# A hybrid mLSTM and chunk-MLP layer on one core: when weight blocks are cut in two parts and when their loads begin

## The chip, the core and the metric

The kernel runs on one core of a Trainium2 chip. The metric is device time in microseconds of one execution, the median over several runs. TensorE (PE in the rows) does the matrix products, with the loading of its stationary operand counted apart (PEld); VectorE (DVE) and ScalarE (ACT) do elementwise work and empty PSUM, GpSimd (POOL) does some elementwise work in SBUF, and SyncE's queue (SP) issues all the DMAs. Each engine takes its own instructions in order; an instruction that has to wait holds back everything behind it on that engine.

## What is computed

One inference step of one layer, on a prompt of 2048 rows of 1024 features and on eight single sample rows. Cut to what matters here:

```
h      = rmsnorm(x)
proj   = h @ w_in                      # 1024 -> 10248 columns: q, k, v, o, z_a, gates, u, vb, z_b, gate_a, gate_b
q, k   = silu(causal_conv(q, k))
hm     = mlstm(q, k, v, ...)           # 4 heads x 256, chunks of 128 rows
y_a    = sigmoid(o) * rmsnorm(hm) * silu(z_a)
y_b    = u * (tril(w_s) @ layernorm(vb) + b_s) * silu(z_b)
merged = sigmoid(gate_a) * (y_a @ w_pa) + sigmoid(gate_b) * (y_b @ w_pb)
x      = x + rmsnorm(merged @ w_out)
x      = x + sigmoid(x @ w_ple_gate) * rmsnorm(p @ w_ple)
```

All of it is in float32, and the matmuls must keep about that precision.

## The kernel before

**Passes, units, products.** The prompt is taken in NP = 4 passes of 512 rows (the sample rows ride along in pass 1). In each pass the big products with weights are 28 units in the order of `PASS`: four times v, qk, og, gg (one head each), four times ub, and two each of pa, pb, wo and wg. Each unit is a product of a 1024 by 512 weight with the pass's 512 rows, done in Strassen's way: 2 by 2 blocks, seven block products in place of eight. A block is 512 by 256 (one SBUF tile of 128 partitions by 1024 floats, 512 KB). The seven products of a unit take the weight blocks in the order A11, A12, S2, S3, S1, A22, S4 (`ORDER`; S1 to S4 are sums of raw blocks). So there are 28 x 7 = 196 products in a pass and 784 in all.

**Cutting.** To keep precision, each operand is cut into a high part (`whi`, a copy by ACT into the type fp32r, line 124) and a low part (`wlo`, block minus high part, by DVE, line 129). A product is 24 matmuls: for each of 4 slices of 128 and each of 2 halves, high x high, high x low, low x high. They stand in `run_unit` at lines 490 (results with rows of x on the partitions) and 493 (the other way round, printed as rhi/whi and so on).

**Where blocks come from.** In pass 0 the raw blocks are loaded, the sums are made by DVE, and all are kept in DRAM. In passes 1 to 3, S2, S1 and S4 (`CUT_KEPT`) are loaded ready cut, as a pair of tiles, high and low. The other four of each unit (A11, A12, S3, A22; "raw blocks" below) are loaded as one raw tile (`wraw`) and cut anew. All these tiles come from one pool of 13 buffers (`w`). A tile is handed the buffer of a tile that was used up; its first write waits until the last reader of that one is done. Buffers are handed out in the order in which tiles are asked for.

**The schedule.** `Stream` holds the list of all products. Just ahead of the matmuls of product t, `run_unit` calls `reach_high(t + 1)`, where `n` is `t + 1`: first the high copies up to product `n + CUT - 1` = t + 2, then the loads up to product `n + LOAD - 1` = t + 7 (in pass 0 up to `n + 4`). In the middle of the product's matmuls it calls `reach_low`, which asks for the low tiles of the high copies just made and has DVE make them. After the product come the copies out of PSUM (`snap` and `consumer`: tiles `s`, `u`, and the names of the results), and then a step of whatever runs beside it (attention, convolution, the cutting of the other operand in `build`, the fetching of it back from DRAM in `from_dram`: tiles `blk`, `rhi`, `rlo`). The tool that builds the program keeps roughly this order on each engine, but may move instructions.

Of the kernel before, what the change touches and what calls it, by code (L numbers as in the profile page):

```python
# [74 lines left out]
def tile_layer(ctx: ExitStack, tc: tile.TileContext, I, O):  # L75
# [46 lines left out]
    def copy(out, in_, scale=None):  # L122
        if scale is None:
            S.activation(out, in_, AF.Copy)  # L124
        else:
            S.activation(out, in_, AF.Copy, scale=scale)
# [129 lines left out]
    class Stream:  # L256


        CUT, SUM, LOAD = 2, 3, 7

        def __init__(self):
            self.items = [(p, u, n) for p in range(NP) for u in PASS for n, *_ in order(u)]
# [58 lines left out]

        def reach_high(self, n):
            end = len(self.items)
            while self.split < min(end, n + self.CUT):
                key = self.items[self.split]
                self.split += 1
                if key in self.ready:
                    continue
                hi = self.tile(key[1], "whi", F32R)
                copy(hi, self.raw[key])  # L330
                self.high[key] = hi
            n = min(n, end - 1)
            while self.loaded < min(end, n + (self.LOAD if self.items[n][0] else 5)):
                self.load(*self.items[self.loaded])
                self.loaded += 1
# [1424 lines left out]
```

## Time and profile before

| what | value |
|---|---|
| median of 3 runs | 2886.32 us (2886.23 to 2891.51) |
| the profiled execution | 2878.66 us, of which the span from first to last instruction 2877.0 us |
| TensorE busy (matmul) | 2703.2 us, 94% of the span |
| VectorE, ScalarE, GpSimd busy | 2143.5, 1540.1, 512.8 us |
| mean DMA rate | 268 GB/s |
| pass 0, passes 1 to 3 in the trace | 0 to 798, 798 to 1553, 1553 to 2213, 2213 to 2877 us |

The pass borders are the starts of the first weight product of each pass, read from the trace. Idle time that a wait shows is that of the engine named first. A row of the waits gives who waited, for whom, the total, how often, and the longest. A row of the timeline gives start, duration, engine, line, operation, tiles, and in brackets the idle time ahead of it with what ended it.

### The profile page before, as it was taken

What the parts mean: (1) busy time and instruction counts of PE and PEld (TensorE: products, weight loads), DVE (VectorE), ACT (ScalarE), POOL (GpSimd) and SP (SyncE); (2) the same over time, 40 slices, a digit from 0 to 9 for tenths busy, and PEclk for the clock granted to TensorE, in tenths of its full rate; (3) what the DMA queues carried; (4) which work ended last, traced back from release to release, by engine and by line L of the source; (5) the groups of instructions that cost most, each with busy time, mean ns of one, the idle gap of its engine ahead of it and who ended that gap; (6) DMA issues with size and microseconds to landing.
All of it is one profiled execution on the core that took longest, in us unless ns stands there. A gap on an engine that the chain in (4) does not pass through costs nothing. (4 is left out here: it accounts for less than half of the span.)

```text
span 2877.0 us, 56022 instructions
## 1 busy us (share of the span) xinstructions
PE 2703.2 (94%) x21835; PEld 2639.0 (92%) x21835; DVE 2143.5 (75%) x3513; ACT 1540.1 (54%) x2668; POOL 512.8 (18%) x557
## 2 busy tenths in 40 slices
PE   6999999888899999999999999999999999999998
PEld 6899989888789899989889999999998999999898
DVE  8888888888977667766868766567678766665767
ACT  5555646445645555544456655564356545554445
POOL 3333332334310000101020100101111010101110
PEclk9999999899999999999999999999999999999999
DMA  6567667867777888889878777779878787788886
GB/s 223 220 249 273 242 235 267 295 253 255 262 257 249 287 267 273 276 272 328 285 250 294 254 260 257 253 258 322 311 277 298 241 268 262 252 272 279 317 283 231
DMA packets 268628, 770.37 MB, mean 268 GB/s; under 512 B 30066, under 2 KB 89338, under 8 KB 268355
## 3 DMA queue, kind: packets, MB, share of 16 engines
q1 hardware_dynamic: 268362, 766.79, 77.0%
q8 instruction: 172, 2.82, 0.4%
q14 instruction: 94, 0.76, 0.1%
HBM read 595.29 MB, written 171.53 MB: 267 GB/s over the span
## 5 line engine op out<-in xcount | busy, mean ns | idle before, releaser
L493 PE MATMUL acc<-rhi,whi 128*128 128x256 f32 (+1 forms) x4480 | 1289.6, 288 | 30.9 <-ACT s L124 8.9
L493 PE MATMUL acc<-rhi,wlo 128*128 128x256 f32 (+1 forms) x4480 | 1276.5, 286 | 43.1 <-DVE wlo L129 34.1
L493 PE MATMUL acc<-rlo,whi 128*128 128x256 f32 (+1 forms) x4480 | 1275.2, 285 | 0.0
L493 PEld LDWEIGHTS acc<-rhi,wlo 128*128 128x128 f32 x4480 | 859.3, 192 | 50.3 <-DVE wlo L129 39.6
L493 PEld LDWEIGHTS acc<-rhi,whi 128*128 128x128 f32 x4480 | 860.2, 192 | 41.6 <-ACT s L124 10.3
L493 PEld LDWEIGHTS acc<-rlo,whi 128*128 128x128 f32 x4480 | 859.4, 192 | 0.0
L129 DVE TENSOR_TENSOR wlo<-wraw,whi 128x1024 fp32r<-128x1024 f32 (+1 forms) x462 | 597.7, 1297 | 179.2 <-PE acc L493 77.2
L124 ACT ACTIVATE whi<-wraw 128x1024 fp32r<-128x1024 f32 (+1 forms) x504 | 530.1, 1055 | 349.6 <-PE acc L493 209.4
L490 PE MATMUL acc<-whi,rhi 128*128 128x256 f32 (+1 forms) x1792 | 517.7, 290 | 20.7 <-ACT rhi L124 6.7
L490 PE MATMUL acc<-wlo,rhi 128*128 128x256 f32 (+1 forms) x1792 | 512.0, 287 | 16.2 <-DVE wlo L129 14.1
L490 PE MATMUL acc<-whi,rlo 128*128 128x256 f32 (+1 forms) x1792 | 511.8, 286 | 6.3 <-DVE rlo L129 6.2
L490 PEld LDWEIGHTS acc<-whi,rhi 128*128 128x128 f32 x1792 | 346.1, 193 | 28.0 <-ACT rhi L124 9.6
L490 PEld LDWEIGHTS acc<-wlo,rhi 128*128 128x128 f32 x1792 | 345.1, 193 | 19.8 <-DVE wlo L129 16.9
L490 PEld LDWEIGHTS acc<-whi,rlo 128*128 128x128 f32 x1792 | 346.3, 193 | 8.2 <-DVE rlo L129 8.2
L124 ACT ACTIVATE u<-acc 128x512 f32<-128x512 f32 (+1 forms) x272 | 138.9, 517 | 209.8 <-PE acc L493 156.8
L129 POOL TENSOR_TENSOR wlo<-wraw,whi 128x512 fp32r<-128x512 f32 (+1 forms) x84 | 149.0, 1794 | 291.6 <-ACT whi L124 209.5
L124 ACT ACTIVATE s<-acc 128x512 f32<-128x512 f32 (+1 forms) x136 | 69.4, 513 | 79.3 <-PE acc L493 47.2
L790 POOL TENSOR_TENSOR so<-so,sz 128x512 f32<-128x512 f32 (+1 forms) x32 | 60.2, 1880 | 289.7 <-ACT so L774 171.9
L1293 POOL TENSOR_TENSOR yb<-yb,ub 128x512 f32<-128x512 f32 (+1 forms) x32 | 57.1, 1799 | 293.8 <-DVE ub L1291 127.0
L241 POOL TENSOR_SCALAR aab<-au 128x2 f32<-128x2 f32 x32 | 8.5, 266 | 481.6 <-DVE au L883 481.6
L869 DVE SCALAR_TENSOR_TENSOR cext<-cext,fst,smp 128x258 f32<-128x258 f32 x128 | 60.5, 479 | 36.1 <-PE smp L806 36.0
L720 POOL COPY halo<-raw 128x3 f32<-128x3 f32 x64 | 27.5, 454 | 284.8 <-DVE raw L139 154.7
(365 smaller groups left out, 3899.0 us busy)
## 6 DMA issues: line engine op xcount, KB each, us to landing
wraw<-in_w_main SPq DMA_DIRECT2D x351, 512.0 KB
xh<-xh SPq DMA_DIRECT2D x32, 512.0 KB
sg<-sgm SPq DMA_DIRECT2D x24, 512.0 KB
gsig<-sg SPq DMA_DIRECT2D x24, 512.0 KB
x<-in_x_prompt SPq DMA_DIRECT2D x16, 512.0 KB
ya<-ya SPq DMA_DIRECT2D x32, 256.0 KB
xr<-in_x_prompt SPq DMA_DIRECT2D x32, 256.0 KB
pg<-pg SPq DMA_DIRECT2D x32, 256.0 KB
```

The lines of the kernel that those rows point to most:

```text
L124: S.activation(out, in_, AF.Copy)
L129: eng.tensor_tensor(lo, full, hi.bitcast(F32), op=ALU.subtract)
L241: G.tensor_scalar(out, ms, EPS, None, op0=ALU.add)
L490: T.matmul(outs[s], x[:, kt, s * P:(s + 1) * P], wt[:, kt, :], start=first, stop=last, skip_group_check=not opens)
L493: T.matmul(outs[s], wt[:, kt, s * P:(s + 1) * P], x[:, kt, :], start=first, stop=last, skip_group_check=not opens)
L720: G.tensor_copy(halo[:, ct, :], x[:, TP:TP + 3])
L790: G.tensor_tensor(so[:, s], so[:, s], sz[:, s], op=ALU.mult)
L869: V.scalar_tensor_tensor(cext[:, h, kt, :], cext[:, h, kt, :], gt.fst[:, h, self.c:self.c + 1], p3, op0=ALU.mult, op1=ALU.add)
L1293: G.tensor_tensor(y[:, :, l, :], y[:, :, l, :], ub[:, :, l, :], op=ALU.mult)
```

## The change

Two numbers of `Stream`'s schedule. In products of passes 1 to 3 the high copies (and with them the low parts) are asked for one product further ahead: up to t + 3 in place of t + 2. And the loads in these passes begin one product less far ahead: up to t + 6 in place of t + 7. Pass 0 keeps its two and its five.

```diff
-        CUT, SUM, LOAD = 2, 3, 7
+        CUT, SUM, LOAD = 2, 3, 6
...
         def reach_high(self, n):
             end = len(self.items)
-            while self.split < min(end, n + self.CUT):
+            while self.split < min(end, n + self.CUT + (self.items[min(n, end - 1)][0] > 0)):
                 key = self.items[self.split]
                 self.split += 1
                 if key in self.ready:
```

No instruction is added or taken away, and the pool keeps its 13 buffers.

## Rows read from the trace of the kernel before

**Rows 1.** The page: span, busy time of the engines, granted clock.

```profile
span 2877.0 us, 56022 instructions
...
PE 2703.2 (94%) x21835; PEld 2639.0 (92%) x21835; DVE 2143.5 (75%) x3513; ACT 1540.1 (54%) x2668; POOL 512.8 (18%) x557
...
PEclk9999999899999999999999999999999999999999
```

**Rows 2.** Busy time by pass: stretch, length, engines (instructions), clock, DMA share, GB/s.

```profile
0.00:798.00 798.00, 696.92 (x5399) 676.73 (x5400) 690.12 (x912) 444.24 (x712) 286.76 (x234) 0.94 0.70 252
798.00:1553.00 755.00, 726.35 (x5819) 694.28 (x5818) 543.30 (x1136) 402.48 (x779) 80.94 (x132) 0.98 0.81 275
1553.00:2213.00 660.00, 642.49 (x5327) 636.96 (x5326) 462.94 (x744) 356.94 (x606) 73.26 (x103) 0.98 0.81 277
2213.00:2877.00 664.00, 637.41 (x5296) 630.98 (x5295) 447.18 (x724) 336.39 (x573) 71.81 (x88) 0.99 0.79 269
```

**Rows 3.** Waits of PE in passes 1 to 3 (798 to 2877).

```profile
PE acc L493 <- DVE wlo L129: 18.2, 14, 3.3
PE smp L1599 <- DVE xq L1591: 6.9, 4, 1.8
PE acc L490 <- DVE wlo L129: 6.2, 5, 3.1
...
PE acc L493 <- ACT u L124: 3.9, 7, 0.7
...
PE acc L493 <- ACT whi L124: 2.1, 2, 1.0
...
PE acc L490 <- DVE rlo L129: 1.5, 2, 1.2
```

**Rows 4.** Waits of DVE, ACT and the SP queue in passes 1 to 3.

```profile
DVE wlo L129 <- PE acc L493: 77.2, 56, 3.9
...
ACT whi L124 <- PE acc L493: 192.0, 109, 5.2
...
SPq L117 <- DVE wlo L129: 515.9, 255, 6.7
SPq L117 <- PE acc L493: 453.7, 276, 5.0
```

**Rows 5.** Instructions on tile wraw: duration min/median/max in ns, first and last start.

```profile
L124 ACT ACTIVATE whi<-wraw x504: 1039/1057/1087, 10.4 to 2853.7; 128x1024 fp32r<-128x1024 f32 x162, 128x1040 fp32r<-128x1040 f32 x6
L129 DVE TENSOR_TENSOR wlo<-wraw,whi x462: 1149/1222/2348, 16.0 to 2855.7; 128x1024 fp32r<-128x1024 f32 x148, 128x1040 fp32r<-128x1040 f32 x6
```

**Rows 6.** DVE and ACT timeline in a regular stretch of pass 1.

```profile
1175.07 1.22 DVE L129 TENSOR_TENSOR wlo<-wraw,whi 128x1024 fp32r<-128x1024 f32 x1 [0.16 <-issue]
...
1178.09 1.23 DVE L129 TENSOR_TENSOR wlo<-wraw,whi 128x1024 fp32r<-128x1024 f32 x1 [0.96 <-PE acc L493]
...
1175.18 1.06 ACT L124 ACTIVATE whi<-wraw 128x1024 fp32r<-128x1024 f32 x1 [2.40 <-PE acc L493]
```

**Rows 7.** Line 493 alone in a dense stretch: length, PE and PEld busy (x), clock, DMA.

```profile
1177.80:1195.30 17.50, 17.50 (x148) 17.50 (x147) 1.00 0.82 276
```

**Rows 8.** PE timeline: waits at the pass border and in three merge stretches.

```profile
812.51 0.58 PE L490 MATMUL acc<-wlo,rhi 128*128 128x260 f32 x1 [3.13 <-DVE wlo L129]
...
1371.14 0.49 PE L493 MATMUL acc<-rhi,wlo 128*128 128x260 f32 x1 [3.31 <-DVE wlo L129]
...
2044.44 0.58 PE L493 MATMUL acc<-rhi,wlo 128*128 128x256 f32 x1 [3.21 <-DVE wlo L129]
...
2712.56 0.48 PE L493 MATMUL acc<-rhi,wlo 128*128 128x256 f32 x1 [1.77 <-DVE wlo L129]
```

**Rows 9.** SP queue, ACT and DVE in the merge stretch of pass 2.

```profile
2030.69 3.75 SPq L117 DMA_DIRECT2D blk<-yb  x4
2034.54 0.40 SPq L117 DMA_DIRECT2D wraw<-in_w_main  x1
...
2039.68 1.06 ACT L124 ACTIVATE rhi<-blk 128x1024 fp32r<-128x1024 f32 x1 [1.59 <-DMA blk<-yb]
...
2040.77 1.22 DVE L129 TENSOR_TENSOR rlo<-blk,rhi 128x1024 fp32r<-128x1024 f32 x1 [4.09 <-ACT rhi L124]
2042.03 1.22 DVE L136 TENSOR_TENSOR blk<-blk 128x1024 f32<-128x1024 f32 x1
2043.17 1.22 DVE L129 TENSOR_TENSOR wlo<-wraw,whi 128x1024 fp32r<-128x1024 f32 x1
```

**Rows 10.** All engines in the merge stretches of passes 2 and 3, columns as in the second group.

```profile
2034.00:2046.00 12.00, 8.34 (x63) 7.93 (x62) 6.58 (x7) 3.66 (x4) 0.00 (x0) 0.90 1.02 414
2701.00:2713.00 12.00, 9.77 (x79) 9.37 (x78) 5.47 (x6) 5.21 (x6) 0.00 (x0) 0.99 1.02 403
```

**Rows 11.** A landing in an ordinary stretch: issue on the SP queue, first use by PE.

```profile
2743.40 0.43 SPq L117 DMA_DIRECT2D prow<-in_p_prompt  x1
...
2748.44 0.41 PE L1454 MATMUL smp<-ident,prow 128*128 128x128 f32 x2 [1.58 <-DMA prow<-in_p_prompt]
```

## The prediction

> **What bounds the kernel now.** I read the page first: PE is busy for 94% of the span, at nine tenths of its clock or more in every slice [rows 1]. So the time is PE's own work plus what PE stands still, and only the second can move here, as no matmul is added or taken away. Next the busy time by pass [rows 2]: in pass 0 PE stands 798.0 - 696.9 = 101 us, in passes 1 to 3 it stands 28.7 + 17.5 + 26.6 = 73 us. The change acts in passes 1 to 3 alone, so 73 us, 2.5% of the time, is all that it could ever win.
>
> Then what PE waits for in those passes [rows 3]. The largest entry is the low part of a weight block: 18.2 us in 14 waits at line 493 and 6.2 us in 5 at line 490, together 24.4 us in 19 waits, none over 3.3 us. The high part costs 2.1 us at line 493. The rest is the chain of the output stage (6.9 us), copies out of PSUM (u, 3.9 us) and the like, which do not hang on the cut.
>
> Why is a low part late? The waits of the other engines [rows 4] show that DVE, ahead of a low part, stood 77.2 us in 56 waits for PE, and ACT, ahead of a high part, 192.0 us in 109. Nothing that these read comes from PE; what they wait for is the buffer to write in, which a product must set free first. A regular stretch shows the rhythm [rows 6]: low parts start 3.02 us apart (1175.07, 1178.09), the second after 0.96 us of standing for PE, and each takes 1.2 us [rows 5]. A product is 24 matmuls; 148 of them took 17.5 us [rows 7], so one product takes 24 x 0.118 = 2.8 us, or 2.9 with the gaps. So a low part starts as a product ends, and the product after the next one needs it one product later: the cushion is 2.9 - 1.2 - 0.2 = 1.5 us (0.2 for handing on). Any delay of DVE beyond 1.5 us stops PE.
>
> **The change, part by part.** *Cutting one product further ahead.* The number of cuts is the same, some 336 in passes 1 to 3 (3 passes, 28 units, 4 raw blocks), with the same 1.06 us on ACT and 1.22 us on DVE [rows 5], so no engine gets more work. Each low part gets one product more before it is needed: the cushion grows from 1.5 to about 4.4 us. A wait of x us today was a low part late by x beyond its cushion, so every wait up to 2.9 us should go and the two of 3.3 and 3.2 us [rows 8] should leave 0.4 and 0.3.
>
> That holds only if the buffers allow it, so I counted the tiles held once a product's requests are made: two for each product that is cut, three for the raw block being cut, and one (raw) or two (pair) for each block loaded ahead. Before: 4 for products t and t + 1, then block t + 2, then five loads. For t = A11, A12, ..., S4 that is 13, 14, 13, 14, 13, 14, 15, on average 13.7, against 13 buffers. That fits the rows: with the pool always full the low parts wait for the end of a product. After: 6 for three cut products, block t + 3, then three loads: 14, 12, 13, 12, 13, 14, 12, on average 12.9. So one load less pays for one cut more. High parts should find a buffer free without waiting for PE, and only two low parts of four (those of S3 and A12) still wait for a product's end, which now leaves them 4.4 us.
>
> So of the 24.4 us, what goes? The wait of 3.13 us at 812.51 [rows 8] stays: it belongs to the second product of pass 1, and the deeper cut begins with requests made at the pass border, too late for it. 24.4 - 3.1 = 21.3. Of these, 3.31 + 3.21 + 1.77 = 8.3 us lie in the three merge stretches [rows 8]. There the low part stood behind a cut of the other operand (`rlo<-blk`), which DVE could not start for 4.09 us because `blk` came late [rows 9]. The low part now goes ahead of that, but the next one ahead may be held by its own load (below), so I take half, 4.1. Of the other 13.0 us I take four fifths, 10.4: where DVE is behind by its own work, what PE meets next is a copy out of PSUM, such as u with waits of up to 0.7 us [rows 3]. Of the 2.1 us for high parts I take half, 1.0. Sum: 4.1 + 10.4 + 1.0 = 15.5 us.
>
> *Loads one product later.* The number of DMAs is the same. On the SP queue each weight load moves one product back, past whatever is asked for in between (attention's rows, gates, `blk`, stores); these gain, for the queue stood 515.9 us for low parts and 453.7 us for PE [rows 4], mostly for buffers of loads asked for too early. A raw block was loaded seven products ahead and copied by ACT two ahead: five products, 14.5 us, for the transfer. Now it is six and three: three products, 8.7 us. The nearest rows for a landing: a small one in an ordinary stretch took 2743.40 to 2748.44, 5.0 us [rows 11]; the first of four 512 KB transfers in a merge stretch, where the DMA share is 1.02, took 2030.69 to 2039.68, 9.0 us [rows 9, 10]. So ordinarily 3.7 us are left and the cost is nothing; in the merge stretches a landing can be 0.3 us late or more. Below: nothing. Above: the third rival. I take nothing beyond the half already given away, as a late copy has the new cushion before PE stops. Pairs loaded ready cut lose a product too, and keep six, 17.4 us, which is far above 9.0.
>
> *Order on the engines.* The builder may move instructions, and a new schedule may be laid out otherwise in places. No row prices that; I put nothing, and it is one reason for the width.
>
> The sum against the profiled execution: 2878.66 - 15.5 = 2863.2 us (its span of 2877.0 would be 2861.5). The median of the runs shown lies 7.7 us above that execution, so for the median 2886.3 - 15.5 = 2870.8, say **2871 us**.
>
> **The rivals.** *The wait comes back as a wait for buffers (nothing gained, 2886 us).* If low parts still get their buffer only as the product before their use ends, the 24.4 us stay. For it: 77.2 us in 56 waits on PE show that buffers, not raw data, held DVE [rows 4]. Against it: the count, 12.9 tiles in place of 13.7. The Trainium skill, Perfetto Trace Analysis, section Optimization Strategy, says that a gap which repeats on the engine that should be full can mean that there isn't enough SBUF for the next tile. By that rule a longer lead in the same 13 buffers would win nothing; the trace agrees that the pool was the brake, but in the count the load depth pays for the lead.
>
> *The time is given back at the next late thing (2881 us).* DVE is busy 543.3 of 755 us in pass 1 and near 70% in passes 2 and 3 [rows 2]. Where it is simply behind, an earlier low part means a later copy out of PSUM, behind it in DVE's queue. If two thirds of the 15.5 us come back so, 5 us are left: 2886.3 - 5 = 2881. For it: DVE worked without a gap from 2040.77 until the low part was done, just ahead of the wait of 3.21 us [rows 8, 9]. Against: it idles for some 30% of these passes.
>
> *Raw blocks land too late (slower, 2896 us).* The point that decides is a landing longer than 8.7 us. Place: the two fetches of an operand in each pass, whose four `blk` transfers of 512 KB now go ahead of a weight load that used to precede them. At 403 GB/s [rows 10] those four take 4 x 0.524 / 403 = 5.2 us, on top of 5.0 [rows 11]: 10.2 us, 1.5 too late. ACT stands in its copy, DVE in the low part behind it, and with them the copies out of PSUM that PE needs for its next bank. On four blocks of each of six fetches that is 24 x 1.5 = 36 us, and the 4.1 us counted as won there are lost as well: 2886.3 - 11.4 + 36 = 2911 if PE pays all, 2893 if it pays half; I put the case at 2896. For it: DMA shares of 1.02 and the 9.0 us [rows 9, 10]. Against: there are only a few such stretches, and PE has the new cushion and other PSUM banks before it has to stop.
>
> **How the numbers follow.** The spread of the runs shown, 2886.23 to 2891.51, is 0.2%, or 5.8 us: less than that cannot be told from no change. Chances: the forecast 0.65, the buffer rival 0.08, given back 0.14, late landings 0.13. The first lies under 2880.5, that is faster: 0.65; the next two are within 0.2%: 0.22; the last is slower: 0.13. The forecast's own range: at best all of 21.3 + 2.1 us goes, and the 3.9 and 1.5 us of u and rlo [rows 3] with it, 28.8 us, 2857; at worst half of the 15.5 comes, 2879. To hold 8 in 10 the range takes in the two cases of no difference and stops short of the slower one: 2857 to 2889.
>
> **What would show it.** Right: in passes 1 to 3, PE's waits for wlo fall from 24.4 to about 5 us, ACT's wait for PE ahead of whi falls well below 192 us, and DVE's ahead of wlo to about half of 77 us; in a regular stretch the low part is done two products ahead of its use. Wrong, by the buffer rival: those waits stay. By the second: wlo goes from PE's list, but u, s or the results take its place. By the third: ACT shows waits for DMA wraw ahead of whi, above all near the fetches of `blk`. The prediction would also be wrong if pass 0 moved, which the change does not touch.

## The result, and the profile after

| | before | after |
|---|---|---|
| median | 2886.78 us (4 runs, 2886.23 to 2891.51) | 2846.93 us (4 runs, 2845.06 to 2847.34) |
| the profiled execution | 2878.66 us | 2845.06 us |
| pass 0 in the trace | 798.2 us | 801.0 us |
| passes 1 to 3 in the trace | 2078.8 us | 2042.3 us |

The ratio is 0.9869 (95% interval 0.9853 to 0.9885): 1.3% or 39.9 us faster, where 15.5 us were forecast. The two traces differ by less, 33.6 us, because the profiled execution of before lay 8.1 us under its median and that of after 1.9 us under its own. Pass 0 moved by 2.8 us, so the whole difference of the traces and a little more, 36.5 us, lies in passes 1 to 3.

The page of after, the lines that answer to [rows 1]:

```profile
span 2843.3 us, 55892 instructions
...
PE 2683.7 (94%) x21835; PEld 2623.8 (92%) x21835; DVE 2136.0 (75%) x3513; ACT 1542.4 (54%) x2666; POOL 494.7 (17%) x557
...
PEclk9999999989999999999999999999999999999999
```

PE still does 21835 matmuls, but is busy 19.5 us less. Nothing was taken away: the same matmuls took less time. The busy time by pass (columns as in [rows 2]; the last row is passes 1 to 3 together):

```profile
801.00:1540.40 739.40, 720.10 (x5818) 689.32 (x5817) 541.10 (x1135) 404.34 (x779) 80.47 (x132) 0.99 0.82 280
1540.40:2189.80 649.40, 634.14 (x5326) 630.28 (x5325) 457.74 (x744) 355.37 (x603) 64.38 (x101) 1.00 0.81 282
2189.80:2843.30 653.50, 632.90 (x5296) 627.80 (x5294) 445.69 (x725) 338.55 (x574) 64.81 (x90) 0.99 0.78 274
801.00:2843.30 2042.30, 1987.14 (x16436) 1947.40 (x16434) 1444.54 (x2601) 1098.26 (x1954) 209.66 (x323) 0.99 0.80 279
```

The last row beside that of the kernel before, same view:

```profile
798.20:2877.00 2078.80, 2006.05 (x16436) 1962.02 (x16434) 1453.22 (x2601) 1095.82 (x1956) 226.01 (x323) 0.99 0.80 274
```

Length less busy time is what PE stands: 72.8 us before, 55.2 us after. So of the 36.5 us, **17.6 us are standing** (the forecast's subject) and **18.9 us are busy time**, with 16436 matmuls in either row. The mean clock of the three passes was 0.98, 0.98 and 0.99 [rows 2] and is 0.99, 1.00 and 0.99.

What is waited for in passes 1 to 3 of after, beside [rows 3, 4]:

```profile
PE acc L490 <- ACT s L124: 6.9, 4, 3.2
PE smp L412 <- DVE xos L1622: 6.6, 2, 5.0
PE acc L490 <- DVE wlo L129: 6.2, 4, 3.0
...
PE acc L493 <- ACT u L124: 5.1, 9, 0.9
PE acc L493 <- DVE wlo L129: 3.0, 5, 1.7
...
ACT whi L124 <- DVE wlo L129: 197.0, 125, 5.0
DVE wlo L129 <- PE acc L493: 88.1, 64, 3.9
```

PE's waits for low parts fell from 24.4 us in 19 to 9.2 us in 9. ACT hardly waits for PE ahead of a high part any more (4.6 us at line 493, for 192.0), but waits 197.0 us for DVE's low parts, as long as it did for PE; and DVE waits for PE ahead of a low part a little longer than before, 88.1 against 77.2 us. Both engines wait as long as before, only earlier.

**Where the busy time went.** Windows of the kernel before, chosen right behind the four waits of [rows 8] (length, PE busy and matmuls first; the clock is the third number from the end):

```profile
811.50:818.30 6.80, 5.79 (x26) 5.57 (x27) 3.65 (x6) 1.56 (x4) 0.00 (x0) 0.50 0.78 308
1371.30:1374.70 3.40, 3.40 (x17) 3.40 (x18) 3.40 (x4) 0.30 (x2) 0.00 (x0) 0.50 1.02 405
2043.70:2053.90 10.20, 8.77 (x39) 8.48 (x40) 8.79 (x9) 5.04 (x6) 0.00 (x0) 0.50 0.71 262
2712.70:2716.10 3.40, 3.40 (x17) 3.40 (x18) 3.40 (x4) 1.06 (x1) 0.00 (x0) 0.50 1.03 418
```

The granted clock is 0.50 there, the lower level of 1.2 GHz: 17 matmuls in 3.40 us, where a matmul every 0.118 us [rows 7] would make 29. The duration of 0.58 us in [rows 8] showed it already; a matmul at full clock is listed with 0.28 us. The same four places in the trace of after:

```profile
811.50:818.30 6.80, 6.80 (x59) 6.77 (x59) 6.36 (x10) 4.55 (x7) 2.09 (x3) 1.00 1.01 365
1360.00:1375.00 15.00, 14.21 (x114) 13.79 (x115) 14.93 (x19) 7.92 (x11) 0.00 (x0) 1.00 0.82 292
2030.00:2042.00 12.00, 11.23 (x90) 10.79 (x91) 11.97 (x14) 6.51 (x7) 0.00 (x0) 1.00 0.96 357
2688.00:2700.00 12.00, 10.34 (x81) 9.53 (x79) 12.00 (x13) 7.57 (x9) 0.00 (x0) 1.00 0.60 223
```

At these four places the long waits are gone, and with them the half clock. Over passes 1 to 3, leaving out the last stretch at the very end of the kernel, the trace of before has 12 stretches at half clock, 57.8 us together, and that of after 6 with 23.8 us. At half clock a stretch does in its length what would take half of it, so at most (57.8 - 23.8) / 2 = 17.0 us of the 18.9 us of busy time are the clock.

These two traces show the clock's part larger than it is on average. A second trace of the same program (after_again, below) has 8 stretches with 37.4 us, at most 10.2 us less loss than before, and is 14.5 us less busy. And the mean granted clock that is listed with every run is 0.9748 over the 41 runs of the kernel before in the experiments and 0.9783 over eight of the change: multiplied by their spans, 72.7 and 61.9 us of full clock were not granted. So the clock is some 11 us of the gain, at most, and what the rest of the busy time is stays open.

### The profile page after: what moved, and what is told of

It reads as the page before. It is cut to its first block, busy times and chain, and to the rows that moved or that the text cites. A ratio compares the mean times of both kernels' runs of the same rounds, so it can differ in the third digit from the quotient of the medians.

```text
span 2843.3 us, 55892 instructions
## 1 busy us (share of the span) xinstructions
PE 2683.7 (94%) x21835; PEld 2623.8 (92%) x21835; DVE 2136.0 (75%) x3513; ACT 1542.4 (54%) x2666; POOL 494.7 (17%) x557
## 5 line engine op out<-in xcount | busy, mean ns | idle before, releaser
L493 PE MATMUL acc<-rhi,whi 128*128 128x256 f32 (+1 forms) x4480 | 1286.8, 287 | 36.5 <-ACT s L124 10.6
L493 PEld LDWEIGHTS acc<-rhi,whi 128*128 128x128 f32 x4480 | 855.1, 191 | 49.3 <-ACT s L124 12.8
L129 DVE TENSOR_TENSOR wlo<-wraw,whi 128x1024 fp32r<-128x1024 f32 (+1 forms) x462 | 593.5, 1288 | 155.4 <-PE acc L493 88.1
L490 PE MATMUL acc<-whi,rhi 128*128 128x256 f32 (+1 forms) x1792 | 516.1, 289 | 19.5 <-ACT s L124 6.9
L790 POOL TENSOR_TENSOR so<-so,sz 128x512 f32<-128x512 f32 (+1 forms) x32 | 51.4, 1605 | 294.2 <-DVE sz L787 209.2
L718 DVE SCALAR_TENSOR_TENSOR q<-raw,vecs,q 128x512 f32<-128x512 f32 x96 | 68.1, 747 | 23.9 <-ACT q L714 23.7
```

The lines of the kernel that those rows point to most:

```text
L129: eng.tensor_tensor(lo, full, hi.bitcast(F32), op=ALU.subtract)
L490: T.matmul(outs[s], x[:, kt, s * P:(s + 1) * P], wt[:, kt, :], start=first, stop=last, skip_group_check=not opens)
L493: T.matmul(outs[s], wt[:, kt, s * P:(s + 1) * P], x[:, kt, :], start=first, stop=last, skip_group_check=not opens)
L718: V.scalar_tensor_tensor(o, x[:, j:j + TP], convw[:, j, ct:ct + 1], o, op0=ALU.mult, op1=ALU.add)
L790: G.tensor_tensor(so[:, s], so[:, s], sz[:, s], op=ALU.mult)
```

## The experiments

Each ratio is to the kernel before as it ran in the same session. Lengths, busy and standing time are those of passes 1 to 3 in the one trace of each kernel, from the same view as above; the wait for low parts is the sum of PE's rows in the waits. The stretches of stand_long and stand_chain hold 24 matmuls more than the others, that of stand_short 72.

| run | median us | ratio (95% interval) | length | PE busy | standing | PE for low parts |
|---|---|---|---|---|---|---|
| before | 2881.93 to 2886.78 in four sessions | | 2078.8 | 2006.1 | 72.8 | 24.4 |
| after | 2846.93 | 0.9869 (0.9853 to 0.9885) | 2042.3 | 1987.1 | 55.2 | 9.2 |
| after_again | 2850.16 | 0.9880 (0.9862 to 0.9899) | 2043.8 | 1991.5 | 52.3 | 8.8 |
| cut2_load6 | 2857.98 | 0.9918 (0.9900 to 0.9935) | 2050.0 | 1992.3 | 57.7 | 19.1 |
| cut3_load7 | 2872.92 | 0.9967 (0.9950 to 0.9984) | 2066.8 | 1998.6 | 68.2 | 12.8 |
| shallow_pa1 | 2856.66 | 0.9915 (0.9898 to 0.9931) | 2048.8 | 1989.0 | 59.8 | 19.9 |
| cut2_load5 | 2854.32 | 0.9893 (0.9876 to 0.9911) | 2044.9 | 1987.1 | 57.8 | 20.2 |
| cut3_load5 | 2841.80 | 0.9850 (0.9832 to 0.9868) | 2034.0 | 1985.7 | 48.3 | 6.6 |
| cut4_load6 | 2856.99 | 0.9906 (0.9888 to 0.9924) | 2052.3 | 1988.4 | 63.9 | 6.3 |
| w12 | 2869.98 | 0.9951 (0.9933 to 0.9970) | 2051.7 | 1990.5 | 61.2 | 7.3 |
| stand_short | 2882.27 | 0.9997 (0.9982 to 1.0013) | 2074.1 | 2002.0 | 72.1 | 8.2 |
| stand_long | 2868.34 | 0.9940 (0.9921 to 0.9959) | 2062.6 | 1997.4 | 65.2 | 8.7 |
| stand_chain | 2916.21 | 1.0104 (1.0086 to 1.0122) | 2104.6 | 2010.9 | 93.7 | 9.0 |

**One half of the change alone: the looser load.**

```diff
-        CUT, SUM, LOAD = 2, 3, 7
+        CUT, SUM, LOAD = 2, 3, 6
```

> Loads six ahead, cuts still two ahead. If the lead of the cut makes the gain: the pool holds 12.3 tiles on average, so low parts start in the middle of a product rather than at its end, the cushion grows by about 1.4 us in place of 2.9, and the time falls by 5 to 15 us, to 2872 to 2882. If the looser pool makes it: 30 to 40 us less, 2847 to 2857, as in the changed kernel.

Measured: 2857.98 us, ratio 0.9918, some 24 us, between the two forecasts. The half that the prediction priced at nothing gives most of the gain. Waits in its trace:

```profile
ACT whi L124 <- PE acc L493: 104.3, 64, 4.6
...
DVE wlo L129 <- PE acc L493: 32.5, 19, 2.6
```

The kernel before has 192.0 us in 109 and 77.2 us in 56 there [rows 4]. One load fewer in the pool, and low parts are made sooner within the same lead: by the trace's times of every raw block in passes 1 to 3, the median from the end of a low part to the start of its product rises from 1.5 us (the prediction's cushion) to 3.6 us. PE's waits for low parts fall only to 19.1 us, but at the pass border and in the merge stretch of pass 2, where [rows 8] have 3.13 and 3.21 us, none is longer than 1.9 us (in that of pass 1 it is 4.0 us); the waits for `xq`, 6.9 us in [rows 3], are 0.9 us; and busy time is 13.7 us less.

**The other half alone: the deeper cut.**

```diff
-            while self.split < min(end, n + self.CUT):
+            while self.split < min(end, n + self.CUT + (self.items[min(n, end - 1)][0] > 0)):
```

> Cuts three ahead, loads still seven ahead: 14.3 tiles wanted on average, 13 there. If the lead makes the gain: 25 to 40 us less than before, 2847 to 2862. If the looser pool makes it: nothing gained or a loss, 2880 to 2895, with low parts waiting for PE more than the 77 us of before.

Measured: 2872.92 us, ratio 0.9967, some 9 us, again between the two forecasts. Waits for low parts are halved (12.8 us), but standing falls by only 4.6 us: by the prediction's way of counting, 14.3 tiles on average are wanted from 13 buffers, and other waits rise. The two halves together give 4.6 + 15.1 = 19.7 us of standing and 7.5 + 13.7 = 21.2 us of busy time, close to the 17.6 and 18.9 us of the whole change.

**The change without the deeper cut in one unit.** In the second `pa` unit, where the merge stretches lie, the cut stays at two ahead.

```diff
+            p, u, _ = self.items[min(n, end - 1)]
-            while self.split < min(end, n + self.CUT + (self.items[min(n, end - 1)][0] > 0)):
+            while self.split < min(end, n + self.CUT + (p > 0 and u != ("pa", 1))):
```

> The changed kernel, but with cuts only two ahead in the second pa unit of passes 1 to 3, where the three merge stretches lie. If a long stand of PE costs its own length and then half speed for a while: the three waits of 3.3, 3.2 and 1.8 us come back with half-clock stretches of 3.4, 10.2 and 3.4 us, so 8.3 + 8.5 = 17 us more than the changed kernel, near 2864. If it costs its length alone: 8 us more, 2855. If what is saved there is lost again behind it: under 3 us, 2847 to 2850.

Measured: 2856.66 us, ratio 0.9915, 6 to 10 us over the two runs of the change. Its PE timeline (lines shifted by one), and the windows behind the first and the last of these waits:

```profile
1364.84 0.59 PE L494 MATMUL acc<-rhi,wlo 128*128 128x260 f32 x1 [3.38 <-DVE wlo L129]
...
2036.00 0.39 PE L494 MATMUL acc<-rhi,wlo 128*128 128x256 f32 x1 [4.19 <-DVE wlo L129]
...
2693.30 0.58 PE L494 MATMUL acc<-rhi,wlo 128*128 128x256 f32 x1 [5.63 <-DVE wlo L129]
...
1364.80:1368.20 3.40, 3.36 (x16) 3.36 (x17) 2.29 (x2) 0.00 (x0) 0.00 (x0) 0.53 1.02 407
2693.30:2703.50 10.20, 9.51 (x46) 9.22 (x47) 9.18 (x9) 3.54 (x4) 0.00 (x0) 0.54 0.65 250
```

The three waits of the merge stretches are back, 13.2 us of them, and each brings a stretch at half clock, of 3.4, 3.4 and 10.2 us. So at these three places it is the deeper cut, not the load, that takes the waits away, and the stretches at half clock come and go with the waits. What these stretches cost does not show in the sums: the time is near what length alone would make (2855), not what half speed on top would make (2864); busy time, 1989.0 us, lies between the two runs of the change, and so does the half clock, with 34.0 us against 23.8 and 37.4.

**The change again, as a control of those below.**

> The changed kernel once more, beside the others. Both theories: 1.2 to 1.5% under the kernel before.

Measured: 2850.16 us, ratio 0.9880, an interval that overlaps that of the first session: 32.6 us under the kernel before of its own session, where the first had 39.9. Below, this run is called the control. Its busy time in passes 1 to 3 is 4.4 us longer than that of after, with the same program: the size of what the clock varies from one execution to the next.

**One buffer less.** The change with 12 buffers.

```diff
-    wp = ctx.enter_context(tc.tile_pool(name="w", bufs=13))
+    wp = ctx.enter_context(tc.tile_pool(name="w", bufs=12))
```

> The changed kernel with 12 buffers in the pool for 12.9 tiles wanted, as far short as the kernel before was with 13 for 13.7. If buffers held too long by early loads made the difference: back by 20 us or more, 2865 or more where the changed kernel has 2845. If only the lead of the cut counts: under 10 us more.

Measured: 2869.98 us, ratio 0.9951, 20 us over the control, about what the first theory asked for. A wait of its trace:

```profile
ACT whi L124 <- PE acc L493: 216.0, 139, 6.9
```

With fewer buffers than the 12.9 tiles wanted, high parts wait for PE again, longer than in the kernel before. PE's waits for low parts stay small (7.3 us), thanks to the lead; what grows is the rest, 61.2 - 7.3 = 53.9 us against 43.5 in the control.

**Does a wait cost more than its length?** Three kernels put waits of PE into the change, ahead of the second product of units in passes 1 to 3, with two transposes that read a copy of `s1`, into the bank that this product opens. In stand_short they read `s1` itself, in 36 units; in stand_long what GpSimd makes of it in one addition, in 12; in stand_chain the last of four such additions in a chain. The three edits drawn together:

```diff
             outs = accs[an][0]
+            if p and wn == "A12" and u[0] in ('gg',):
+                held = tmp([P, 2, 256], "held")
+                G.tensor_tensor(held, s1[:, :, 0:256], s1[:, :, 0:256], op=ALU.add)
+                for _ in range(3):                                   # stand_chain alone
+                    more = tmp([P, 2, 256], "held")
+                    G.tensor_tensor(more, held, held, op=ALU.add)
+                    held = more
+                for o in outs:
+                    T.transpose(o[:, 0:P], held[:, 0, 0:P], ident)
             xh, xl = res.hi[bn], res.lo[bn]
```

> The changed kernel with about the same standing in 36 pieces of 0.8 us (ahead of A12 in the qk, og and gg units of passes 1 to 3, for a copy by ACT alone), 29 us in all. If the length alone counts: 25 to 35 us more than the changed kernel, as with the long ones. If short stands bring no half clock: the same 25 to 35 us, but far under the long ones' 50 to 70 us.

Measured: 2882.27 us, 32 us over the control. Standing rises by 19.8 us: 21.8 us of waits for `s` at the transposes, 27 of them, none over 2.0 us. Busy time rises by 10.5 us with 72 matmuls more, and there are no more stretches at half clock than in the control; one of the 27 waits, of 1.8 us, had one behind it. So these short waits cost about their length.

> The changed kernel with PE made to stand at 12 places (ahead of A12 in the gg units of passes 1 to 3), for a copy by ACT of 0.6 us and an addition by GpSimd of 1.9 us, about 2.6 us each, 31 us in all. If a stand costs its own length alone: 25 to 35 us more than the changed kernel, and no more half-clock time than its 15 us lost in passes 1 to 3. If a stand of this length also brings a stretch at half clock: 12 more such stretches of 3.4 us or more, 1.7 us or more lost in each, so 50 to 70 us more.

Measured: 2868.34 us, 18 us over the control. The long waits did not come about: PE was given other work in the meantime and waited 8.6 us for `held` in all. So this run says nothing of long waits, and serves as the base of the next: at the 12 places PE waits 0.6 to 1.1 us, and at none of them does a stretch at half clock follow.

> The changed kernel with twelve long stands of PE put in: ahead of the second product of the gg units of passes 1 to 3, four GpSimd copies in a chain on the emptied bank (1.33 us each in the run with one of them), and then two transposes of the last copy into the bank which that product opens. The run with one copy cost 18 us over the changed kernel with PE waiting 0.4 us at a time and no half-clock stretch more. Theory of length alone: three more copies add 12 x 4.0 = 48 us of standing, so some 66 us over the changed kernel, 2914 to 2920 us, and the half-clock time lost in passes 1 to 3 stays at 14 to 20 us. Theory of the clock: waits of 3 to 5 us are followed by stretches at half clock as at the three merge stretches of the kernel before (3.4 to 10.2 us long, so 1.7 to 5 us lost each), so 20 to 50 us come on top: 2935 to 2965 us, lost clock 40 to 70 us. If PE is given other work in the meantime, neither comes about and the run says nothing.

Measured: 2916.21 us, ratio 1.0104. The total lies where the theory of length alone put it, but not by its sum: 48 us of standing more were expected, and 9.1 us of the difference between the two traces lie in pass 0, which the edit does not touch. The trace, first two windows of stand_long, passes 1 to 3 and 3.4 us behind a put-in wait of 0.56 us:

```profile
803.80:2866.40 2062.60, 1997.43 (x16460) 1953.65 (x16458) 1458.80 (x2601) 1099.39 (x1954) 224.06 (x335) 0.99 0.81 276
1708.40:1711.80 3.40, 3.40 (x29) 3.40 (x30) 2.54 (x4) 0.71 (x2) 1.41 (x4) 1.00 0.44 169
```

and then those of stand_chain, with two of 3.4 us right behind put-in waits and one ahead of one:

```profile
812.90:2917.50 2104.60, 2010.93 (x16460) 1967.57 (x16458) 1461.46 (x2601) 1100.35 (x1954) 269.24 (x371) 0.98 0.78 270
1735.50:1738.90 3.40, 3.40 (x19) 3.40 (x18) 1.38 (x3) 1.91 (x2) 0.82 (x4) 0.51 0.00 0
1824.00:1827.40 3.40, 2.71 (x23) 2.51 (x22) 1.23 (x1) 1.77 (x3) 2.45 (x3) 1.00 0.94 339
1831.10:1834.50 3.40, 3.39 (x16) 3.40 (x17) 1.91 (x4) 1.44 (x2) 1.35 (x4) 0.50 0.00 0
```

PE's matmuls there, and its wait for `held` in all:

```profile
1831.11 0.69 PE L483 MATMUL acc<-ident,held 128*128 128x128 f32 x2 [3.02 <-POOL held L480]
...
1833.94 0.41 PE L502 MATMUL acc<-rhi,wlo 128*128 128x256 f32 x1
1834.15 0.41 PE L502 MATMUL acc<-rhi,whi 128*128 128x256 f32 x1
...
1835.28 0.28 PE L502 MATMUL acc<-rhi,wlo 128*128 128x256 f32 x1
1835.39 0.28 PE L502 MATMUL acc<-rhi,whi 128*128 128x256 f32 x1
```

```profile
PE acc L483 <- POOL held L480: 37.3, 12, 3.6
```

Against stand_long, with 16460 matmuls in either, standing is 93.7 - 65.2 = 28.5 us longer and busy time 2010.93 - 1997.43 = 13.5 us. Behind every one of the 12 put-in waits, of 3.0 to 3.6 us, the clock is at half for 3.4 us (once 6.8): the matmuls start 0.21 us apart until 1834.4, then 0.12 us. Twelve such stretches are 44.2 us, at most 22.1 us of loss. So a long wait does cost more than its length: the two kernels differ only in three more additions by GpSimd ahead of the same transposes. It costs less than the theory of the clock said for this run, and its 13.5 us on 28.5 us are less than the 18.9 us that went with 17.6 us in the change. Nine of the 12 carried no DMA at all, while the four shown of the kernel before ran at DMA shares of 0.71 to 1.03: what they have in common is the wait ahead of them.

**How far the two numbers can be turned.** First the changed kernel with loads one product later still:

```diff
-        CUT, SUM, LOAD = 2, 3, 6
+        CUT, SUM, LOAD = 2, 3, 5
```

> The changed kernel with loads begun one product later still (five ahead in place of six), high copies as in the change. Tiles held fall to 11.4 on average against 13 buffers; a raw block has two products, 5.8 us, from the issue of its load to its high copy. Theory that the pool is what is left: DVE's waits for PE ahead of a low part fall well below 88 us, and the time is that of the changed kernel or up to 10 us less (2838 to 2850). Rival, late landings: landings of 4.5 us at the median but up to 11 us now reach ACT; its waits for the load ahead of a high copy rise from some 9 us to over 60, and the time is 5 to 30 us above the changed kernel.

Measured: 2841.80 us, ratio 0.9850: the fastest of all, though its interval overlaps that of the change. Each theory was half right. ACT does wait for raw blocks to land now, 144.7 us in all, of which the largest row is

```profile
ACT whi L124 <- DMA wraw<-in_w_main: 106.6, 51, 6.3
DVE wlo L129 <- PE acc L493: 88.8, 62, 4.3
```

but PE does not feel it, since the low part has three products to come through; one wait of 4.26 us for a low part, at 2683.56, is the exception. DVE's wait for PE did not fall, so it measures no harm by itself. Next the cut four ahead, the loads as in the change:

```diff
-            while self.split < min(end, n + self.CUT + (self.items[min(n, end - 1)][0] > 0)):
+            while self.split < min(end, n + self.CUT + 2 * (self.items[min(n, end - 1)][0] > 0)):
```

> The changed kernel with high copies of passes 1 to 3 asked for four products ahead in place of three, loads as in the change. Tiles held rise to 13.4 on average, above the pool's 13 again, and the load has two products. Theory that the lead is what counts: the waits of PE for low parts fall from 9 us to under 5 and the time by up to 5 us. Rival, the buffers: high copies wait for PE and low parts longer than 197 us, loads go out later, and the time is 5 to 20 us above the changed kernel, most of it without a wait of PE for a low part.

Measured: 2856.99 us, ratio 0.9906, 7 to 10 us over the two runs of the change. PE's waits for low parts are 6.3 us, but the rest of the standing grows, 6.8 us of it in two waits for `zb`, which DVE writes; DVE was busy without a gap in the 12 us ahead of both. The time is the rival's, but its sign is absent: high copies wait less for PE and low parts than in the change, 150 for 221 us. They wait 151.6 us for raw blocks to land, but so they do in cut3_load5, the fastest run. With loads six ahead, more lead than three buys nothing; a cut four ahead with later loads was not tried. Last the kernel before with loads five ahead, the cut at two (`CUT, SUM, LOAD = 2, 3, 5`):

> The kernel before with loads begun five products ahead in place of seven, cuts two ahead as before. Tiles held fall to some 10.7 on average, so no low part should wait for a buffer; a raw block still has three products, 8.7 us, for its load. Going from seven to six gained 24 us. Theory that the buffers alone were the brake: five gains a little more than six (2845 to 2858 us), and PE's waits for low parts go below the 19 us that were left with six. Rival, the lead: with the cut still two products ahead a low part that DVE makes late stops PE as before; those waits stay at 15 to 20 us and the time stays at that of the kernel with six (2855 to 2865 us).

Measured: 2854.32 us, ratio 0.9893, against 0.9918 with six, their intervals overlapping. The time agrees with the first theory and the low parts with the second: PE still waits 20.2 us for them. The median low part is done 5.0 us ahead of its product here, nearly as early as in the change, so those waits are a matter of the few late ones, and only a longer lead takes them away. DVE's wait for PE ahead of a low part is back at 72.2 us, from 32.5 us with six, although by the count two buffers are free: that row is no gauge of how full the pool is.

By the prediction's way of counting tiles, the runs with a cut three ahead order by what the pool has to spare: 11.4 tiles for 13 buffers 2842 us, 12.9 for 13 some 2847 to 2850, 12.9 for 12 2870, 14.3 for 13 2873 us. Only the step between the second and the third is larger than the intervals of the ratios.

## Why the prediction was right and wrong

The direction was right, and so was the mechanism for the waits on low parts. The size was not: 15.5 us were forecast, and 39.9 us came, 36.5 us of them in passes 1 to 3 of the traces. Two terms that the sum put at nothing, PE's own busy time and the later loads, carry most of the difference.

- **The step that failed** is the first: PE is at nine tenths of its clock or more in every slice, so "only the second can move here, as no matmul is added or taken away". Busy time did move, by 18.9 us with the same 16436 matmuls (14.5 us in the control), and at most 17.0 us of it (10.2) are the clock. A tenth-wide digit of a slice of 72 us hides a stretch of 3.4 us at half clock (and one slice, in pass 0, shows an 8), and the sum priced each wait at its own length. The clock column of [rows 2] had the loss in it: 0.98, 0.98 and 0.99 over 755, 660 and 664 us are some 35 us of full clock not granted. The 0.58 us in [rows 8] was a sign too, quoted but not read. That the clock falls with long waits is shown: the put-in waits of stand_chain and the returned ones of shallow_pa1 brought it down. How much each wait costs is not settled: 0.5 us for each us in stand_chain, 1.1 or 0.7 in the two traces of the change. Four of the 12 stretches at half clock of the kernel before stand beside no wait of 1.7 us or more but beside shorter ones, of 0.98 to 1.52 us, while other waits of up to 1.84 us have none; so the length of one wait isn't the whole story.
- **The waits for low parts** came out near their sum, in part by luck: 14.5 us of 24.4 were to go, 15.2 us went, but in other places. The 3.13 us at the pass border, "too late for it", went too; cut2_load6 removed it without any deeper cut. In the merge stretches 0.46 and 1.68 us are left of those waits in passes 2 and 3 and 0.2 us in pass 1, so some 6 of the 8.3 us went, not 4.1. Of the other 13.0 us some 6 went, not 10.4.
- **Loads one product later**, priced at nothing, are worth 24 us alone. The count of tiles had the cause in it (one load less pays for one cut more), but only as what the deeper cut needs; it has its own gain, as low parts at the old lead are also made sooner. That this comes through the pool is argued: w12 shows that one buffer less costs the changed kernel 20 us, but the kernel before with 14 buffers was not tried.
- **The high parts** were to find a buffer free. They hardly wait for PE any more, but 197.0 us for a low part of DVE; that this is the buffer of a raw block which the low part sets free is read from the order of the requests and was not tried. DVE's wait for PE was to fall to half of 77.2 us and rose to 88.1 us; the prediction read it as the pool being full, but cut2_load5 and cut3_load5 have 72.2 and 88.8 us of it with buffers to spare, so what it is stays open. PE's waits fell all the same: the median from a finished low part to its product is 5.3 to 5.4 us in the two traces of the change, where 4.4 was forecast and 1.5 was before.
- **The buffer rival** fell for this change. Yet w12 and cut3_load7 show it at work: where the tiles exceed the buffers, most of the gain goes. The Trainium skill, Perfetto Trace Analysis, section Optimization Strategy, says that a gap which repeats on the engine that should be full can mean that there isn't enough SBUF for the next tile. The trace of w12 agrees, with 61.2 us of standing for the control's 52.3; but a longer lead in the same 13 buffers did not win nothing, as the prediction took from it: cut3_load7 won 9 us.
- **Given back at the next late thing** happened in part: PE's waits outside low parts fell by only 2.4 us (72.8 - 24.4 = 48.4 to 55.2 - 9.2 = 46.0), and new ones such as 3.0 us for `mt` stand among them.
- **Late landings** were no danger: ACT's waits for a raw block to land, ahead of a high part, rose from 2.4 to 12.6 us, and even 144.7 us in cut3_load5 did not slow the kernel.

Open is 3.4 us between the 39.9 us of the medians and the 36.5 us of the traces; pass 0, whose schedule is the same, varied between 798 and 813 us over the traces.

## What to carry to other kernels

Price a long stand of TensorE with what comes behind it: look at the granted clock and the matmul durations right after each wait of some 3 us, not at the mean of a slice, and give busy time its own term even when no work is added or removed. In a shared pool, count the tiles that lead and prefetch ask for together: loads begun too early take the buffers that the near work needs, and beginning them later was the larger gain here. A wait of an engine that is not the bound can stay as long as it was and still cease to matter, if it comes one product earlier.

## What the runs showed of the hardware

The granted clock fell to its lower level of 1.2 GHz at each of twelve waits of 3.0 to 3.6 us that were put in, at none of twelve waits of 0.6 to 1.1 us in the same places, and at one of 27 of up to 2.0 us (0.8 us on average). The lower clock lasted 3.4 us mostly, at times 6.8 or 10.2 us. In the kernel before, 12 such stretches in passes 1 to 3 cost up to half of 57.8 us, 1.0% of its time, and no entry of the waits shows any of it.
